# New PSUM banks for the last pair's sums, and three engines instead of two on mixer B's first queries

## The chip, the cores and the metric

The kernel runs on one core of one Trainium2 chip. The metric is the device time of one execution in microseconds (us); the median of several runs counts. The engines are TensorE (PE, matrix products, with its weight loads shown as PEld), VectorE (DVE), ScalarE (ACT), GpSimd (POOL) and SyncE (SP, which here issues the weight DMAs). Every engine works through its own queue in order and waits there for the other engines.

## The reference

Two layers of an encoder over 256 tokens of width 2048: layer 0 with mixer A (grouped-query attention), layer 1 with mixer B (three groups of heads with windows and dilations), each followed by a gated MLP of inner width 5632 with a convolution of width 3 in it, and a final norm.

```
def reference(x, ...):
    h = x
    for i in range(DEPTH):                      # 2
        hn = rms_norm(h, mix_norm[i])
        h = h + (mixer_a if i % 2 == 0 else mixer_b)(hn, ...)
        h = h + conv_ffn(rms_norm(h, ffn_norm[i]), w_up[i], conv_w[i], conv_b[i], w_down[i])
    return rms_norm(h, final_norm)

def mixer_b(h, w_qkv, w_o, rel_bias):           # 3 groups of 8 heads of 128
    qkv = (h @ w_qkv).reshape(b, s, 3, 3, 8, 128)
    for g in range(3):
        o, lz = dilated_group(q[g], k[g], v[g], rel_bias[g], window[g], dilation[g])
        ...
    return concat(softmax(log_zs)[g] * outs[g]) @ w_o

def conv_ffn(h, w_up, conv_w, conv_b, w_down):
    gate, val = split(depthwise_conv3(h @ w_up) + conv_b)
    return (silu(gate) * val) @ w_down
```

## The kernel before

All weights stream from HBM in blocks of 128 x 1024 float32 (`raw`, loaded from SP's queue, six buffers). Products are made in PE's reduced float32 format with a high and a low part: `split_raw` has ACT round a block to its high half `wh` (line 128) and DVE subtract it for the low half `wl` (line 129); both sit in a short ring of buffers. Each block is used by matmuls with `wh` and then with `wl`, so that PE needs a `wh` when it begins a block and a `wl` some matmuls later. The activations stand on the other side in the same two parts.

**Accumulators.** PSUM has eight banks of 128 x 512 float32, called b0 to b7. Some of the products are made by a seven-product scheme (Strassen-like) over two column blocks n0 and n1 and the two halves of 128 tokens: `project_pair` takes a list of `units`, one per weight block, either ("c", ...), a common block that goes into two of the four sums C11, C21 (column block n0) or C12, C22 (n1), or ("P", ...), one of the seven products. Products 1, 5, 6, 7 have accumulators of their own, M1, M5, M6, M7, and are added by `combine` on DVE and ACT (lines 475 to 487); products 2, 3 and 4 go straight into C11, C12 and C21. At the end `done` adds C11, C21 and then C12, C22 to the residual stream `h` (line 649). Which bank each of the eight takes is written out in `project_pair` (lines 221 to 223): the i-th name of `place` takes the i-th bank of the list, and b is the same for consecutive pairs.

```
            place = ("M1", "M5", "M6", "M7", "C11", "C21", "C12", "C22")
            b = bank_at[0]
            acc = {k: bank((4, 5, 6, 7, 2 - b, 3 - b, b, b + 1)[i], "acc") for i, k in enumerate(place)}
```

The last MLP (layer 1) does its down-projection in two halves `hf` over the inner width; in the second, `pair(0, 1, ...)` and then `pair(2, 3, ..., tail=True)` are the last matmuls of the program. The units of the tail begin with four common blocks that go into C11 and C21, then product 1, and C12 and C22 come late. A new tile in a bank waits for the last reader of the tile before it.

**Mixer B's queries.** Each half `hf` of the heads (four heads of every group) goes through groups g = 0, 1, 2. `seven` makes keys and queries with the same scheme; `k_gen` and `s_gen` are generators that are advanced one piece at a time between the weight blocks, so their instructions are interleaved with the block splits in the queues of ACT, DVE and POOL. For the queries, ACT scales the sums into `stg` (line 797), DVE turns 32 x 32 blocks in `tT` (line 348), and `place_blocks` puts sixteen pieces of 32 x 256 where they belong: the letter of `place` for each of four partition groups says which engine copies (p is POOL, line 358; a is ACT, line 360; v is DVE, line 362). For group 0 the placed queries are then split into `qTh` (ACT, line 303) and `qTl` (DVE, line 304) for the score matmuls.

A scheduler sets the final order within each queue; block splits have priority over what surrounds them.

Of the kernel before, what the change touches and what calls it, by code (L numbers as in the profile page):

```python
# [33 lines left out]
def tile_encoder(ctx: ExitStack, tc: tile.TileContext, x, xT, w_a, w_ao, q_gain, k_gain, w_b, w_bo,  # L34
# [180 lines left out]
    def project_pair(w, n0, n1, lhs, forms, units, late, early_done, n0_done, product_done=None, tail=False,  # L215
                     lazy=False):
        home = {1: "M1", 2: "C11", 3: "C12", 4: "C21", 5: "M5", 6: "M6", 7: "M7"}
        if product_done or lazy:
            acc = dict(zip(("C11", "C21", "C12", "C22"), new_acc() + new_acc()))
        else:  # L220
            place = ("M1", "M5", "M6", "M7", "C11", "C21", "C12", "C22")
            b = bank_at[0]
            acc = {k: bank((4, 5, 6, 7, 2 - b, 3 - b, b, b + 1)[i], "acc") for i, k in enumerate(place)}

        def touched(u):
            return (home[u[2]],) if u[0] == "P" else (("C11", "C21"), ("C12", "C22"))[u[2] // 2]

        first, last = {}, {}
        for i, u in enumerate(units):
            for k in touched(u):  # L230
                first.setdefault(k, i)
                last[k] = i
        if tail:
            last["C12"] = last["C22"] = None
        blocks = {}
        sums = {5: ("11", "12"), 7: ("12", "22"), 6: ("22", "11"), 4: ("21", "22")}

        def block(kg, b):
            if (kg, b) not in blocks:
                blocks[kg, b] = load_raw(w, (n0, n1)[int(b[1]) - 1], kg, int(b[0]) - 1)  # L240
            return blocks[kg, b]

        def prepare(u):
            kind, kg, p = u
            if kind == "P" and p in sums:
                dst, src = (block(kg, b) for b in sums[p])
                with tc.high_priority(offset=AHEAD):
                    nc.vector.tensor_tensor(dst, dst, src, ALU.add)  # L248
                if p == 6:
                    done_raw(blocks.pop((kg, "11")))  # L250
                elif p == 4:
                    done_raw(blocks.pop((kg, "22")))

        last_s = max(i for i, u in enumerate(units) if u[0] == "P")
        for i, (kind, kg, p) in enumerate(units):
            if i == late:
                drain()
            if kind == "c":
                r = load_raw(w, (n0, n1)[p // 2], kg, p % 2)
            else:  # L260
                b = {1: "11", 2: "21", 3: "22", 5: "11", 7: "12", 6: "22", 4: "21"}[p]
                r = block(kg, b)
            if i + 1 < len(units):
                prepare(units[i + 1])
            wh, wl = split_raw(r, kind == "c" or p in (7, 4))
            if kind == "P" and p in (7, 4):
                blocks.pop((kg, b))
            todo = []
            if kind == "c":
                for j in range(2):  # L270
                    for m, k in enumerate(touched((kind, kg, p))):
                        todo.append((k, *at(lhs[4 * kg + 2 * (p % 2) + j], m), j))
            else:
                f = forms(kg)[p]
                for j in range(2):
                    x = f[j] if isinstance(f, list) else [t[:, j * P:(j + 1) * P] for t in f]
                    todo.append((home[p], *x, j))
            for k, *_ in todo:
                if k not in acc:
                    acc[k] = bank(4 + ("M1", "M5", "M6", "M7").index(k), "acc") if lazy else ps_tile()  # L280
            fresh = {k for k in acc if first[k] == i}
            for k, xh, xl, j in todo:
                nc.tensor.matmul(acc[k], xh, wh[:, j, :], start=k in fresh, stop=False)  # L283
                fresh.discard(k)
                nc.tensor.matmul(acc[k], xl, wh[:, j, :], start=False, stop=False)  # L285
            todo.sort(key=lambda t: (t[0], t[3]))
            for k, xh, xl, j in todo:
                nc.tensor.matmul(acc[k], xh, wl[:, j, :], start=False, stop=last[k] == i and j == 1)  # L288
            if product_done and kind == "P" and home[p][0] == "M":
                product_done(home[p], acc.pop(home[p]))  # L290
            if i == last_s:
                early_done(acc)
            if i == max(last["C11"], last["C21"]):
                n0_done(acc)
            if not (product_done or lazy) or kind == "c" or p in (1, 5, 7, 4):
                step()
        return acc
# [521 lines left out]
    def heads_T_dve(o, s, pool, tag, place="pava", more=False):  # L819
        hi, lo = o  # L820
        dst = hi if lo is None else s.rearrange("p m c -> p (m c)").rearrange("p (j t) -> p j t", j=4)
        yield from turned(dst, s, pool, tag, place)
        yield
        if more:
            yield
        if lo is not None:
            split(hi, lo, dst)
# [209 lines left out]
    def mixer_b(hT, ss_in):  # L1037
        with tc.tile_pool(name="bpool", bufs=1) as bp:
# [26 lines left out]
            for hf in range(2):  # L1065
# [15 lines left out]
                def s_gen(g, accs, bts, nmx=nmx, lsum=lsum, nmv=nmv, probs=probs, e=e, kTs=kTs):  # L1081
                    qs = evac_scaled(bp, accs, rstd)
                    yield
                    yield
                    kT, qT = kTs[g], pair_tile(bp, [P, 4, NT], "qT", 1, g > 0)
                    yield from heads_T_dve(qT, qs, bp, "vl", "papa", g == 0)
                    W = NT if g == 0 else P
                    if g < 2:
                        yield
                    for i in range(4):  # L1090
                        yield
                        s = ps_tile()
                        for m in range(2):
                            ks_ = (allp, i) if g == 0 else (allp, i, slice(m * P, (m + 1) * P))
                            mm3(s[:, m * W:(m + 1) * W], qT, kT, (allp, i, slice(m * P, (m + 1) * P)), ks_,
                                True, True)
                        lg = bp.tile([P, 2, NT], F32, tag="lg", name=nm("lg"), bufs=2)
                        lgv = lg[:, :, :W]
                        b = bts[i] if g == 0 else bts[i][:, None, :].to_broadcast([P, 2, P])
                        nc.vector.scalar_tensor_tensor(lgv, s[:, :2 * W].rearrange("p (m c) -> p m c", m=2),  # L1100
                                                       SCALE, b, ALU.mult, ALU.add)
                        nc.vector.tensor_reduce(nmv[:, g, :, i], lgv, axis=AX.X, op=ALU.max, negate=True)
                        sl = (2 * g + 1) * 4 + i
                        if g == 0:
                            pr = [hpool.tile([P, NT], F32, tag=f"a{c}{sl}", name=nm("pr")) for c in "hl"]
                        else:
                            pt = hpool.tile([P, NT], F32, tag=f"ah{sl}", name=nm("pr"))
                            pr = [pt[:, :P], pt[:, P:], pt]
                        for m in range(2):
                            c = 4 * m + i  # L1110
                            nc.scalar.activation(pr[m], lg[:, m, :W], AF.Exp, bias=nmx[:, g, c:c + 1],
                                                 accum_out=lsum[:, g, c:c + 1])
                        probs.append(pr)
                    if g < 2:
                        return
                    mn = small.tile([P, 8], F32, tag="mn", name=nm("mn"))
                    nc.vector.tensor_tensor(mn, nmx[:, 0, :], nmx[:, 1, :], ALU.min)
                    nc.vector.tensor_tensor(mn, mn, nmx[:, 2, :], ALU.min)
                    nc.vector.tensor_tensor(e, mn[:, None, :].to_broadcast([P, 3, 8]), nmx, ALU.subtract)
                    nc.scalar.activation(e, e, AF.Exp)  # L1120
                    nc.vector.tensor_tensor(lsum, lsum, e, ALU.mult)
                    nc.vector.tensor_tensor(mn, lsum[:, 0, :], lsum[:, 1, :], ALU.add)
                    nc.vector.tensor_tensor(mn, mn, lsum[:, 2, :], ALU.add)
                    nc.vector.reciprocal(mn, mn)
                    nc.vector.tensor_tensor(e, e, mn[:, None, :].to_broadcast([P, 3, 8]), ALU.mult)
# [219 lines left out]
```

## Time and profile before

| | us |
|---|---|
| median of 3 runs | 2241.69 (2239.77 to 2242.25) |
| profiled execution, its own time | 2239.69 |
| span of that execution, first to last instruction | 2237.8 |
| PE busy in it | 2223.3 |

A row of a timeline gives start and duration in us, engine, line, operation, output<-inputs, sizes and a count of like instructions in a row; in square brackets is the time for which the engine sat idle before it and what ended that. A row of the waits gives the waiting instruction, what it waited for, and the total, the number and the longest of these waits.

### The profile page before, as it was taken

Reading aid. Unit: us, or ns where it says so; the run is one execution under the profiler, and the core shown is the slowest. Engines: PE = TensorE matmul, PEld = TensorE weight load, DVE = VectorE, ACT = ScalarE, POOL = GpSimd, SP = SyncE. Lnnn points to the kernel's source line nnn. Section 1 sums busy time; section 2 is a strip of 40 time slices with the busy share of each in tenths; the row PEclk is TensorE's granted clock in tenths of the full one; section 3 lists DMA queues with packets and bytes.
Section 4 is the critical chain, followed back from the end, with each engine's and each line's share of the span. In section 5 each row is a group of like instructions: output and inputs, shape, how many; then the busy total and the mean of one; then the engine's idle time right before and its main releaser. Section 6 shows DMA issues by size and latency. Waiting matters only on the chain.

```text
span 2237.8 us, 29101 instructions
## 1 busy us (share of the span) xinstructions
PE 2223.3 (99%) x10033; PEld 1841.7 (82%) x10033; DVE 1806.2 (81%) x2461; ACT 1540.7 (69%) x2373; POOL 339.6 (15%) x490
## 2 busy tenths in 40 slices
PE   9999999999999999999999999999999999999998
PEld 7888888888888888888888888888888888888886
DVE  6777778888878788979887888786887898688897
ACT  7665677777547777767876777576777755677764
POOL 2210212210001010012431313010110100001110
PEclk9999999999999999999999999999999999999999
DMA  8444657766655655666555565565665666555654
GB/s 302 164 146 152 207 189 207 246 200 190 216 196 188 199 188 179 227 203 214 197 185 187 163 206 178 187 199 190 192 194 193 193 207 207 188 193 193 225 190 140
DMA packets 126499, 437.43 MB, mean 195 GB/s; under 512 B 17312, under 2 KB 18080, under 8 KB 126352
## 3 DMA queue, kind: packets, MB, share of 16 engines
q1 hardware_dynamic: 119744, 425.64, 57.9%
q0 software_dynamic: 6176, 9.39, 1.7%
q8 instruction: 78, 1.28, 0.2%
q14 instruction: 69, 0.57, 0.1%
q10 hardware_dynamic: 432, 0.56, 0.1%
HBM read 429.20 MB, written 6.29 MB: 195 GB/s over the span
## 4 chain that ended last, share of the span: by engine, by line
PE 93%; DVE 2%; POOL 2%; issue 1%; ACT 1%; DMA 1%; SPq 0%; DVEq 0%; POOLq 0%; ACTq 0%
PE acc L154 19%; PE acc L155 19%; PE acc L153 19%; PE acc L283 10%; PE acc L285 10%; PE acc L288 10%; POOL stg L358 1%; DVE wl L129 1%; PE ps L318 1%; PE ps L322 0%; POOL pp L358 0%; PE ps L321 0%; PE ps L320 0%; ACT wh L128 0%; PE ps L285 0%
## 5 line engine op out<-in xcount | busy, mean ns | idle before, releaser
L129 DVE TENSOR_TENSOR wl<-raw,wh 128x1024 fp32r<-128x1024 f32 x855 | 1051.5, 1236 | 298.2 <-ACT wh L128 294.7
L128 ACT ACTIVATE wh<-raw 128x1024 fp32r<-128x1024 f32 x855 | 899.3, 1057 | 489.3 <-PE acc L155 198.9
L154 PE MATMUL acc<-wl,xh 128*128 128x512 f32 x1792 | 698.1, 390 | 0.7 <-DVE wl L165 0.4
L153 PE MATMUL acc<-wh,xh 128*128 128x512 f32 x1792 | 698.5, 390 | 0.1
L155 PE MATMUL acc<-wh,xh 128*128 128x512 f32 x1792 | 697.8, 389 | 0.0
L154 PEld LDWEIGHTS acc<-wl,xh 128*128 128x128 f32 x1792 | 336.5, 188 | 71.4 <-DVE wl L165 1.7
L155 PEld LDWEIGHTS acc<-wh,xh 128*128 128x128 f32 x1792 | 336.4, 188 | 69.5
L153 PEld LDWEIGHTS acc<-wh,xh 128*128 128x128 f32 x1792 | 336.4, 188 | 69.0 <-ACT wh L164 0.5
L283 PE MATMUL acc<-wh,ah 128*128 128x512 f32 x762 | 296.9, 390 | 1.5 <-DVE h L649 1.5
L285 PE MATMUL acc<-wh,al 128*128 128x512 f32 x762 | 296.7, 389 | 0.0
L358 POOL COPY u<-t 32x256 f32<-32x256 f32 x176 | 110.9, 630 | 1003.4 <-DVE t L540 995.3
L288 PE MATMUL acc<-wl,ah 128*128 128x512 f32 x762 | 211.8, 389 | 0.0
L283 PEld LDWEIGHTS acc<-wh,ah 128*128 128x128 f32 x762 | 143.0, 188 | 31.6 <-DVE h L649 1.9
L288 PEld LDWEIGHTS acc<-wl,ah 128*128 128x128 f32 x762 | 143.0, 188 | 29.7
L285 PEld LDWEIGHTS acc<-wh,al 128*128 128x128 f32 x762 | 143.0, 188 | 29.5
L360 ACT ACTIVATE u<-t 32x256 f32<-32x256 f32 x352 | 147.7, 420 | 14.0 <-DVE t L540 6.2
L283 PE MATMUL acc<-wh,xh 128*128 128x512 f32 x312 | 122.4, 392 | 1.1 <-ACT wh L128 1.1
L285 PE MATMUL acc<-wh,xh 128*128 128x512 f32 x312 | 121.5, 390 | 0.0
L248 DVE TENSOR_TENSOR raw<-raw,raw 128x1024 f32<-128x1024 f32 x84 | 103.4, 1231 | 12.3 <-DMA raw<-in_w_down_dram 11.5
L288 PE MATMUL acc<-wl,xh 128*128 128x512 f32 x312 | 84.9, 390 | 0.0
L154 PE MATMUL acc<-wl,ah 128*128 128x512 f32 x216 | 84.2, 390 | 0.3 <-DVE wl L129 0.3
L153 PE MATMUL acc<-wh,ah 128*128 128x512 f32 x216 | 84.2, 390 | 0.0
(244 smaller groups left out, 2264.8 us busy)
## 6 DMA issues: line engine op xcount, KB each, us to landing
raw<-in_w_up_dram SPq DMA_DIRECT2D x352, 512.0 KB, 4.4
raw<-in_w_down_dram SPq DMA_DIRECT2D x176, 512.0 KB, 4.8
raw<-in_w_b_dram SPq DMA_DIRECT2D x144, 512.0 KB, 4.5
raw<-in_w_bo_dram SPq DMA_DIRECT2D x48, 512.0 KB, 4.5
raw<-in_w_a_dram SPq DMA_DIRECT2D x40, 512.0 KB, 4.5
raw<-in_w_ao_dram SPq DMA_DIRECT2D x32, 512.0 KB, 3.8
raw<-in_w_a_dram SPq DMA_DIRECT2D x16, 256.0 KB, 6.2
h<-in_x_dram SPq DMA_DIRECT2D x4, 512.0 KB, 8.4
```

The source lines that it names most:

```text
L128: nc.scalar.activation(wh, r, AF.Copy)
L129: nc.vector.tensor_tensor(wl, r, wh.bitcast(F32), ALU.subtract)
L153: nc.tensor.matmul(accs[m], xh, wh[:, j, :], start=st, stop=False)
L154: nc.tensor.matmul(accs[m], xh, wl[:, j, :], start=False, stop=False)
L155: nc.tensor.matmul(accs[m], xl, wh[:, j, :], start=False, stop=sp)
L248: nc.vector.tensor_tensor(dst, dst, src, ALU.add)
L283: nc.tensor.matmul(acc[k], xh, wh[:, j, :], start=k in fresh, stop=False)
L285: nc.tensor.matmul(acc[k], xl, wh[:, j, :], start=False, stop=False)
L288: nc.tensor.matmul(acc[k], xh, wl[:, j, :], start=False, stop=last[k] == i and j == 1)
L318: nc.tensor.matmul(o, lh[ls], rh[rs], start=start, stop=stop)
L358: nc.gpsimd.tensor_copy(dst, src)
L360: nc.scalar.activation(dst, src, AF.Copy)
```

## The change

Two edits. In the tail pair the eight names take the banks in another order: C11, C12, C21, C22 go to b4 to b7, where the pair before kept M1, M5, M6, M7, and the products M1, M5, M6, M7 go to the banks that held C11, C21, C12, C22. And for group 0 of mixer B the queries' placement is "pava" instead of "papa": four of the eight pieces that POOL copied are copied by DVE, in each half of the heads.

```
             place = ("M1", "M5", "M6", "M7", "C11", "C21", "C12", "C22")
+            if tail:
+                place = ("C11", "C12", "C21", "C22", "M1", "M5", "M6", "M7")
             b = bank_at[0]
...
                     kT, qT = kTs[g], pair_tile(bp, [P, 4, NT], "qT", 1, g > 0)
-                    yield from heads_T_dve(qT, qs, bp, "vl", "papa", g == 0)
+                    yield from heads_T_dve(qT, qs, bp, "vl", "papa" if g else "pava", g == 0)
```

All line numbers after line 221 grow by two. SP's order is unchanged.

The first places are in PE's queue, at the start of the tail pair. The accumulators acc_19562 to acc_19569 are created in the order of `place`, so that before the change 19562 is M1, 19566 C11 and 19567 C21:

```order
L283 MATMUL acc_19566<-wh_19572,ah_17520 128x512
L285 MATMUL acc_19566<-wh_19572,al_17521 128x512
L283 MATMUL acc_19566<-wh_19572,ah_17522 128x512
L285 MATMUL acc_19566<-wh_19572,al_17523 128x512
L283 MATMUL acc_19567<-wh_19572,ah_17520 128x512
L285 MATMUL acc_19567<-wh_19572,al_17521 128x512
```

In the same place after the change 19562 is C11 and 19564 is C21:

```order
L285 MATMUL acc_19562<-wh_19572,ah_17520 128x512
L287 MATMUL acc_19562<-wh_19572,al_17521 128x512
L285 MATMUL acc_19564<-wh_19572,ah_17520 128x512
L287 MATMUL acc_19564<-wh_19572,al_17521 128x512
L285 MATMUL acc_19562<-wh_19572,ah_17522 128x512
L287 MATMUL acc_19562<-wh_19572,al_17523 128x512
```

C21's first matmul moved from the fifth to the third place of the block.

The second place is DVE's queue in the first half of the heads, from the turning of group 0's queries (stg_9266 are the queries, tT_9318 their turned blocks) to the low half qTl_9317. Before:

```order
L348 STREAM_TRANSPOSE tT_9318<-stg_9266 128x512 x2
L129 TENSOR_TENSOR wl_9350<-raw_9347,wh_9349 128x1024
L304 TENSOR_TENSOR kTl_9208<-stg_9186,kTh_9207 128x1024
L129 TENSOR_TENSOR wl_9372<-raw_9369,wh_9371 128x1024
L248 TENSOR_TENSOR raw_9347<-raw_9347,raw_9401 128x1024
L129 TENSOR_TENSOR wl_9390<-raw_9387,wh_9389 128x1024
L129 TENSOR_TENSOR wl_9405<-raw_9399,wh_9404 128x1024
L248 TENSOR_TENSOR raw_9401<-raw_9401,raw_9466 128x1024
L129 TENSOR_TENSOR wl_9423<-raw_9347,wh_9422 128x1024
L304 TENSOR_TENSOR qTl_9317<-stg_9266,qTh_9316 128x1024
```

After:

```order
L350 STREAM_TRANSPOSE tT_9318<-stg_9266 128x512 x2
L364 COPY stg_9266<-tT_9318 32x8x32 x2
L129 TENSOR_TENSOR wl_9350<-raw_9347,wh_9349 128x1024
L306 TENSOR_TENSOR kTl_9208<-stg_9186,kTh_9207 128x1024
L129 TENSOR_TENSOR wl_9372<-raw_9369,wh_9371 128x1024
L129 TENSOR_TENSOR wl_9390<-raw_9387,wh_9389 128x1024
L250 TENSOR_TENSOR raw_9347<-raw_9347,raw_9401 128x1024
L129 TENSOR_TENSOR wl_9405<-raw_9399,wh_9404 128x1024
L364 COPY stg_9266<-tT_9318 32x8x32 x2
L250 TENSOR_TENSOR raw_9401<-raw_9401,raw_9466 128x1024
L129 TENSOR_TENSOR wl_9423<-raw_9347,wh_9422 128x1024
L306 TENSOR_TENSOR qTl_9317<-stg_9266,qTh_9316 128x1024
```

Four copies came in, two at the start and two ahead of the last sum of blocks, and wl_9390 moved ahead of one such sum. ACT's queue is the same as before here.

The third place is DVE's queue in the second half of the heads (stg_11194 are the queries). Before, wl_11318 follows wl_11300:

```order
L248 TENSOR_TENSOR raw_11275<-raw_11275,raw_11329 128x1024
L129 TENSOR_TENSOR wl_11300<-raw_11297,wh_11299 128x1024
L129 TENSOR_TENSOR wl_11318<-raw_11315,wh_11317 128x1024
L304 TENSOR_TENSOR qTl_11245<-stg_11194,qTh_11244 128x1024
L129 TENSOR_TENSOR wl_11333<-raw_11327,wh_11332 128x1024
```

After:

```order
L250 TENSOR_TENSOR raw_11275<-raw_11275,raw_11329 128x1024
L129 TENSOR_TENSOR wl_11300<-raw_11297,wh_11299 128x1024
L364 COPY stg_11194<-tT_11246 32x8x32 x4
L129 TENSOR_TENSOR wl_11318<-raw_11315,wh_11317 128x1024
L306 TENSOR_TENSOR qTl_11245<-stg_11194,qTh_11244 128x1024
```

All four copies came in between these two. POOL's queue has four copies instead of eight at both places. Between the first place's queries and the next group a few more instructions swap neighbours on DVE and ACT (a row maximum and a low half, an exponential and a block split).

## The prediction

> **What bounds the kernel now.** I read the page first (engine totals, clock row), then the engine's waits, then the timelines around each wait.
>
> ```profile
> PE 2223.3 (99%) x10033; PEld 1841.7 (82%) x10033; DVE 1806.2 (81%) x2461; ACT 1540.7 (69%) x2373; POOL 339.6 (15%) x490
> PEclk9999999999999999999999999999999999999999
> PE acc L283 <- DVE h L649: 1.5, 1, 1.5
> PE acc L283 <- ACT wh L128: 1.1, 2, 1.0
> PE ps L322 <- DVE qTl L304: 0.6, 1, 0.6
> PE acc L154 <- DVE wl L129: 0.5, 2, 0.3
> ```
>
> TensorE (PE) is busy 2223.3 of a span of 2237.8 us at a full granted clock. Nothing makes the kernel shorter except fewer matmuls, which this change doesn't bring, or shorter waits of PE. The last four rows are PE's waits (total, times, longest). The first, 1.5 us, is what the bank edit speaks to; the second, 1.1 us in two places, is what the placement edit speaks to. The other two are elsewhere (the qTl one is mixer A's). So the change can't win more than a few microseconds, and the question is whether the two waits go in full and whether the work moved to VectorE (DVE) makes a new one.
>
> **The bank edit.** It moves no instruction between engines; it renames where eight accumulators live in the last pair of the second layer's second down-projection half. C11, the first sum that PE starts there, and C21, the second, are named acc_19566 and acc_19567 before, acc_19562 and acc_19564 after (the rows of PE's order are shown with the change). The products still start at the fifth weight block; only the first four blocks' sums sit in other banks, and C21 now starts at once behind C11. The timeline of PE and DVE at that place:
>
> ```profile
> 2174.68 0.39 PE L283 MATMUL acc<-wh,ah 128*128 128x512 f32 x1
> 2174.91 0.39 PE L285 MATMUL acc<-wh,al 128*128 128x512 f32 x1
> 2176.76 0.50 PE L283 MATMUL acc<-wh,ah 128*128 128x512 f32 x1 [1.47 <-DVE h L649]
> 2177.11 0.40 PE L285 MATMUL acc<-wh,al 128*128 128x512 f32 x1
> 2170.17 0.68 DVE L478 TENSOR_TENSOR cu<-acc,cu 128x512 f32<-128x512 f32 x1
> 2176.04 0.67 DVE L649 TENSOR_TENSOR h<-acc,h 128x512 f32<-128x512 f32 x1
> 2180.63 0.68 DVE L649 TENSOR_TENSOR h<-acc,h 128x512 f32<-128x512 f32 x1
> 2190.28 2.35 DVE L129 TENSOR_TENSOR wl<-raw,wh 128x1024 fp32r<-128x1024 f32 x2
> 2186.91 0.39 PE L283 MATMUL acc<-wh,ah 128*128 128x512 f32 x1
> 2194.17 1.07 PE L288 MATMUL acc<-wl,ah 128*128 128x512 f32 x4
> ```
>
> Matmuls start 0.23 us apart (2174.68, 2174.91). C21's first starts 1.85 after its predecessor, 1.62 too many, and the next follows by 0.35, 0.12 too many: 1.74 us. It waits for the L649 at 2176.04, which reads the preceding pair's C21, whose bank it takes. After the change C21 takes the bank of that pair's M6, last read by L478, which ends at 2170.85, almost 4 us before PE comes there. What is late next? M1, M5, M6 and M7 now take the banks of the old C11, C21, C12, C22, the last of which is read by the L649 that ends at 2181.31; M1, the first of the four, starts at 2186.91, 2185.2 in the new time, so nothing waits. The low halves wl that PE needs next are ready early: the tightest in this stretch ends at 2191.50 (2190.28, two in 2.35, 1.22 each, so the first at 2190.28 + 1.22) and PE comes to it at 2194.17, 2.67 later, more than the 1.74 by which PE moves up. Gain 1.74; at least the 1.47 idle that the row itself shows. I take 1.74.
>
> **The placement edit, first half of the heads.** A quarter of the sixteen-block placement of group 0's queries changes hands: 4 of POOL's 8 copies go to DVE, in each half of the heads. ACT's 8 and SP's queue stay as they are; POOL's next issue is a bias DMA that waits for DVE's use of the old bias long after. By the order shown with the change, in DVE's queue
> two copies stand ahead of all eight tensor-tensor steps that end with wl_9423, a low half that PE waits for, and two ahead of the last two of these.
>
> ```profile
> 1018.83 4.54 POOL L358 COPY stg<-tT 32x256 f32<-32x256 f32 x8 [34.16 <-DVE tT L348]
> 1024.77 9.75 POOL L358 COPY stg<-tT 32x256 f32<-32x256 f32 x8 [1.40 <-DVE tT L348]
> 1030.17 2.75 DVE L129 TENSOR_TENSOR wl<-raw,wh 128x1024 fp32r<-128x1024 f32 x2
> 1034.18 1.42 DVE L129 TENSOR_TENSOR wl<-raw,wh 128x1024 fp32r<-128x1024 f32 x1
> 1036.79 2.35 DVE L129 TENSOR_TENSOR wl<-raw,wh 128x1024 fp32r<-128x1024 f32 x2
> 1032.78 1.06 ACT L128 ACTIVATE wh<-raw 128x1024 fp32r<-128x1024 f32 x1
> 1034.55 1.06 ACT L303 ACTIVATE qTh<-stg 128x1024 fp32r<-128x1024 f32 x1 [0.71 <-POOL stg L358]
> 1035.51 1.99 ACT L128 ACTIVATE wh<-raw 128x1024 fp32r<-128x1024 f32 x2
> 1035.82 0.63 PE L288 MATMUL ps<-wl,sf 128*128 128x512 f32 x2
> 1036.61 0.50 PE L283 MATMUL acc<-wh,xh 128*128 128x512 f32 x1 [0.16 <-ACT wh L128]
> 1036.94 0.39 PE L285 MATMUL acc<-wh,xh 128*128 128x512 f32 x1
> L362 DVE COPY u<-t x176: 283/378/449, 294.0 to 2126.7; 32x256 f32<-32x256 f32 x176
> 217.03 1.12 DVE L362 COPY tM<-tT 32x256 f32<-32x256 f32 x3
> 217.13 2.65 POOL L358 COPY tM<-tT 32x256 f32<-32x256 f32 x4 [42.07 <-DVE tT L348]
> ```
>
> The chain: POOL's eight copies end at 1034.52, ACT's qTh waits for them (0.71), ACT's next weight split stands behind it, and PE waits for that: 1036.61 against 1035.82 + 2 x 0.23, 0.33 too late, and 0.10 on the next start: 0.43 us. POOL's copies took 9.75 us here and 4.54 with DVE less in the way; and DVE's steps are slowed in turn: two of them 2.75 us with POOL at work (1.34 from start to start), 2.35 without (1.13), 0.21 each.
> After: DVE gets four copies of 0.378 (the median, 0.283 to 0.449), 1.51. POOL's four run two beside DVE's copies and two beside tensor-tensors, so 2 instead of 7 of these are slowed: -1.05 (only three fewer: -0.63). The first copy needn't wait for a weight split: -0.07. Net +0.39 (+0.01 to +1.10). wl_9423 ended at 1035.60, so now 1035.99, and PE wants it at 1035.82: a new wait of 0.17 and a restart of about 0.10. The old wait goes: POOL is done by about 1028.3 (1024.77, two copies at 0.43, two at 1.34), DVE's last copies about 2.3 before wl_9423's end, at 1033.7, ACT's split at 1033.84; qTh starts some 0.7 sooner and so does the split behind it. Gain 0.43 - 0.27 = 0.16, range +0.43 to -0.55.
>
> **The second half of the heads.** Here DVE has room: all four copies stand together between wl_11300 and wl_11318.
>
> ```profile
> 1228.88 8.11 POOL L358 COPY stg<-tT 32x256 f32<-32x256 f32 x8 [1.64 <-DVE tT L348]
> 1232.94 1.41 DVE L129 TENSOR_TENSOR wl<-raw,wh 128x1024 fp32r<-128x1024 f32 x1
> 1235.49 1.23 DVE L129 TENSOR_TENSOR wl<-raw,wh 128x1024 fp32r<-128x1024 f32 x1 [1.14 <-ACT wh L128]
> 1234.40 1.06 ACT L128 ACTIVATE wh<-raw 128x1024 fp32r<-128x1024 f32 x1
> 1237.02 1.06 ACT L303 ACTIVATE qTh<-stg 128x1024 fp32r<-128x1024 f32 x1 [1.55 <-POOL stg L358]
> 1237.98 1.04 ACT L128 ACTIVATE wh<-raw 128x1024 fp32r<-128x1024 f32 x1
> 1237.51 0.61 PE L288 MATMUL acc<-wl,xh 128*128 128x512 f32 x2
> 1239.07 0.50 PE L283 MATMUL acc<-wh,xh 128*128 128x512 f32 x1 [0.95 <-ACT wh L128]
> 1239.41 0.40 PE L285 MATMUL acc<-wh,xh 128*128 128x512 f32 x1
> ```
>
> PE loses 1239.07 - 1237.51 - 2 x 0.23 = 1.10 and 0.11 on the next start, 1.21. DVE idles 1.14 us from 1234.35 on, so the copies (1.51) end at 1235.86 and push wl_11318 by 0.37, to about 1237.1; PE wants it at 1237.51. POOL's four are done by 1233.3. qTh starts at 1235.9 instead of 1237.02, the split behind it starts 0.96 later and takes 1.04: 1237.9, when PE wants it at 1237.97. Gain 1.21; with copies of 0.449 the split is 0.2 late and 0.9 is left.
>
> The row at 217.03 is the nearest to this mix: three DVE copies in 1.12 us beside POOL's copies, 0.37 each, no more than the median taken. The Trainium skill speaks against this edit ("Perfetto Trace Analysis", section "Optimizing Scalar/DVE Operations"): GpSimd and VectorE share an SBUF read port, so moving work between those two might not help. By the rows the sum below is 3.1; by that rule the placement is worth nothing and it is 1.7. The trace agrees with the sharing (9.75 us against 4.54) and not with "might not help" where DVE idles.
>
> **Sum.** 1.74 + 0.16 + 1.21 = 3.1 us (1.47 + 0.9 - 0.55 = 1.8 to 1.74 + 0.43 + 1.21 = 3.4). The profiled execution took 2239.69 us, so 2236.6 for it. The runs shown, 2239.77, 2241.69 and 2242.25, lie above it; from their median it is 2238.6, from the middle of all four executions (2240.7) 2237.6. I take 2238.1, between the two (that is 2241.2 - 3.1).
>
> **Rivals.**
> - The placement gives nothing: POOL and DVE take turns, so that the queries are placed no sooner, or DVE's copies make wl late by what POOL's cost before. For it: DVE is filled without a gap in the first half; against it: its 1.14 idle in the second. Only 1.74 is left: 2241.2 - 1.74 = 2239.5.
> - The bank edit doesn't remove its wait, because another reader of a bank is late. Against it is L478's end at 2170.85. Left is 1.4: 2239.8.
> - Slower: DVE's copies are held as POOL's were beside tensor-tensors, 1.3 us each (9.75 for eight). Then 5.2 us stand in DVE's queue in either half: in the first wl_9423 is 3.9 late (5.2 - 1.05 - 0.07 less the 0.22 it had to spare), 3.5 net of the old wait; in the second the copies end at 1239.55 and qTh starts 2.5 later than now. 3.5 + 2.5 - 1.74 = 4.3 slower: 2245.5. It takes copies of some 0.8 us to outweigh the 1.74; no row of this shape on DVE is above 0.449.
>
> **Chances.** Forecast 0.65, placement worthless 0.18, bank wait kept 0.07, slower 0.05, something larger than the sum 0.05. The three runs shown lie within 0.11%, so 0.2%, 4.5 us, is about what a measurement can tell from no change. The sum alone doesn't reach it, but the median shown lies 1 us above the middle of the executions, so that the forecast can show up as over 4.5 us below it about one time in three: faster 0.65 x 0.33 + most of 0.05 = 0.25, slower 0.05, same 0.70. The range goes from 3.4 off the fastest execution, 2236.3, to the rivals that keep half the gain off the highest run, 2240.8, with 0.4 at either end for so few runs.
>
> **What would show it.** The wait for L649 is gone and C21 starts 0.23 behind C11. POOL shows 4 copies at both places, ACT's qTh idles no more for POOL, the two waits on ACT's wh are gone and a small one on wl stands in the first half. Wrong would be: DVE copies over 0.45 us, a wl wait over 0.5 at either place, or a longer tail after the last matmul.

## The result, and the profile after

| | before | after |
|---|---|---|
| median of 14 runs each | 2240.47 us | 2236.84 us |
| lowest and highest | 2238.75 to 2242.94 | 2235.73 to 2238.25 |
| profiled execution, and its span | 2239.69, 2237.8 | 2236.83, 2235.0 |

The ratio is 0.9982, 95% interval 0.9974 to 0.9989: 0.18% faster, a difference clear of the noise, and smaller than the 0.2% that the prediction took for the least that shows. It was 2238.1 predicted; 2236.84 is inside its range.

The engines' totals and PE's waits after the change (engine, line, what it waited for; total, times, longest). L649 of before is L651 now, L478 is L480, and so on: two lines came in above.

```profile
PE 2222.7 (99%) x10033; PEld 1842.6 (82%) x10033; DVE 1805.4 (81%) x2469; ACT 1540.1 (69%) x2373; POOL 330.3 (15%) x482
PE acc L154 <- DVE wl L129: 0.8, 2, 0.6
PE ps L324 <- DVE qTl L306: 0.6, 1, 0.6
```

The two waits of the prediction, for the L649 and for ACT's wh, are gone from the list; VectorE has eight instructions more (2461 to 2469) and POOL eight fewer. The timeline of PE and DVE at the tail:

```profile
2173.22 0.39 PE L285 MATMUL acc<-wh,ah 128*128 128x512 f32 x1
2173.44 0.39 PE L287 MATMUL acc<-wh,al 128*128 128x512 f32 x1
2173.67 0.39 PE L285 MATMUL acc<-wh,ah 128*128 128x512 f32 x1
2173.90 0.39 PE L287 MATMUL acc<-wh,al 128*128 128x512 f32 x1
2169.83 0.68 DVE L480 TENSOR_TENSOR cu<-acc,cu 128x512 f32<-128x512 f32 x1
2175.70 0.68 DVE L651 TENSOR_TENSOR h<-acc,h 128x512 f32<-128x512 f32 x1
2152.76 1.23 DVE L250 TENSOR_TENSOR raw<-raw,raw 128x1024 f32<-128x1024 f32 x1 [0.80 <-DMA raw<-in_w_down_dram]
```

C11's first matmul starts at 2173.22, C21's at 2173.67, 0.23 behind the one ahead of it. M6's reader (L480) was done at 2170.51. The reader of old C21 (the L651) ends at 2176.38: in this execution, in the order of before (C21 fifth, 0.91 behind C11), the old bank would have held PE for 2.3 us, not for the 1.62 in the trace of before. VectorE is later against TensorE here, and the last row shows where: it stood 0.80 us for a weight block.

The first half of the heads, POOL, DVE, ACT and PE:

```profile
1025.15 3.62 POOL L360 COPY stg<-tT 32x256 f32<-32x256 f32 x4 [1.40 <-DVE tT L350]
1025.12 0.69 DVE L364 COPY stg<-tT 32x256 f32<-32x256 f32 x2
1033.28 0.59 DVE L364 COPY stg<-tT 32x256 f32<-32x256 f32 x2
1035.04 1.22 DVE L129 TENSOR_TENSOR wl<-raw,wh 128x1024 fp32r<-128x1024 f32 x1
1034.14 1.04 ACT L305 ACTIVATE qTh<-stg 128x1024 fp32r<-128x1024 f32 x1
1036.00 0.39 PE L287 MATMUL ps<-wh,sf 128*128 128x512 f32 x1
1036.31 0.74 PE L290 MATMUL ps<-wl,sf 128*128 128x512 f32 x2
1036.89 0.40 PE L285 MATMUL acc<-wh,xh 128*128 128x512 f32 x1
```

POOL's four end at 1028.77 (1028.3 was predicted), ACT's qTh idles no more, and wl_9423 ends at 1036.26, so that PE starts 0.31 after its predecessor instead of 0.23: the small new wait.

The second half of the heads:

```profile
1229.12 4.40 POOL L360 COPY stg<-tT 32x256 f32<-32x256 f32 x4 [1.64 <-DVE tT L350]
1234.63 1.18 DVE L364 COPY stg<-tT 32x256 f32<-32x256 f32 x4
1235.85 1.23 DVE L129 TENSOR_TENSOR wl<-raw,wh 128x1024 fp32r<-128x1024 f32 x1
1235.93 1.06 ACT L305 ACTIVATE qTh<-stg 128x1024 fp32r<-128x1024 f32 x1 [0.22 <-DVE stg L364]
1236.90 1.04 ACT L128 ACTIVATE wh<-raw 128x1024 fp32r<-128x1024 f32 x1
1237.76 0.62 PE L290 MATMUL acc<-wl,xh 128*128 128x512 f32 x2
1238.22 0.40 PE L285 MATMUL acc<-wh,xh 128*128 128x512 f32 x1
```

qTh waits 0.22 for VectorE instead of 1.55 for POOL, the split behind it ends at 1237.94, and PE takes it at 1238.22 without a wait.

TensorE issues the same 10033 matmuls in both kernels, so each one's start, less its start in the trace of before, says where time was won. Where that offset moves (times of before):

| place | offset ahead | behind | won |
|---|---|---|---|
| program start to 925.9 | 0.00 | 0.06 | -0.06 |
| 926.6, L154 waits for a low half (a place that the change leaves alone) | 0.06 | 0.40 | -0.34 |
| 1035.8 to 1036.9, first half of the heads | 0.40 | 0.18 | 0.22 |
| 1239.1 to 1239.4, second half | 0.25 | -0.96 | 1.21 |
| 2176.8 to 2177.1, tail | -1.01 | -2.76 | 1.75 |

The three places give 3.18, where the prediction's terms give 3.11, and stretches that the change doesn't touch take 0.4 back; between the places the offset drifts by less than 0.1. The medians differ by 3.63. Is that chance, or is a term larger than its one profiled execution shows?

### The profile page after: what moved, and what is told of

Read it like the earlier page. It is cut to its first block, busy times and chain, and to the rows that moved or that the text cites. A ratio compares the mean times of both kernels' runs of the same rounds, so it can differ in the third digit from the quotient of the medians.

```text
span 2235.0 us, 29102 instructions
## 1 busy us (share of the span) xinstructions
PE 2222.7 (99%) x10033; PEld 1842.6 (82%) x10033; DVE 1805.4 (81%) x2469; ACT 1540.1 (69%) x2373; POOL 330.3 (15%) x482
## 4 chain that ended last, share of the span: by engine, by line
PE 96%; DVE 2%; issue 1%; POOL 1%; DMA 1%; ACT 0%; SPq 0%; DVEq 0%; POOLq 0%; ACTq 0%
PE acc L154 19%; PE acc L155 19%; PE acc L153 19%; PE acc L285 11%; PE acc L287 11%; PE acc L290 11%; PE ps L320 1%; DVE wl L129 1%; PE ps L290 0%; PE ps L287 0%; PE ps L285 0%; PE ps L324 0%; POOL pp L360 0%; PE ps L323 0%; PE ps L322 0%
## 5 line engine op out<-in xcount | busy, mean ns | idle before, releaser
L154 PE MATMUL acc<-wl,xh 128*128 128x512 f32 x1792 | 698.0, 390 | 0.6 <-DVE wl L165 0.3
L154 PEld LDWEIGHTS acc<-wl,xh 128*128 128x128 f32 x1792 | 336.5, 188 | 70.5 <-DVE wl L129 1.3
L154 PE MATMUL acc<-wl,ah 128*128 128x512 f32 x216 | 84.2, 390 | 0.6 <-DVE wl L129 0.6
```

The costliest lines, as they stand in the source:

```text
L154: nc.tensor.matmul(accs[m], xh, wl[:, j, :], start=False, stop=False)
```

## Experiments

### Each edit alone

The bank edit alone puts `"papa"` back for all groups:

```
-yield from heads_T_dve(qT, qs, bp, "vl", "papa" if g else "pava", g == 0)
+yield from heads_T_dve(qT, qs, bp, "vl", "papa", g == 0)
```

> Only the bank edit; the queries stay half on POOL, half on ACT at both places. My theory: C21 of the last pair starts 0.23 us behind its predecessor, PE's wait on the L651 (L649 before) that reads the preceding pair's C21 is gone, and this alone brings 1.74 us of the changed kernel's; PE's two waits on ACT's wh beside the queries stay as before (0.16 and 0.95 idle). Span 2237.8 - 1.7 = 2236.1. Rival, that the two edits hang together (work that VectorE took over shifts it against TensorE until the end): the tail gains less than 1.2 or more than 2.2 us without the placement.

It took 2238.44 (median of 11) against 2241.09 for before on the same chip, ratio 0.9985 (0.9976 to 0.9994), span 2236.4. Its trace wins 1.75 at the tail, as expected, and nothing at the other two places. PE's wait for the old bank is gone and the second half's is there:

```profile
PE acc L285 <- ACT wh L128: 0.9, 1, 0.9
```

But the medians differ by 2.65, almost a microsecond more than the 1.7. The interval of the ratio, 1.3 to 5.4 us, holds both numbers, so that the medians alone can't settle it.

The placement alone keeps the last pair's banks:

```
-if tail:
+if False:
```

> Only the placement edit; the last pair's banks as before. My theory: TensorE gains 0.2 us at the first half of the heads and 1.2 at the second, and then keeps the tail's wait for the reader of old C21; span 2237.8 - 1.4 = 2236.4. Rival 1, that the gain is given back at the tail: if VectorE doesn't move up with TensorE there, the tail's wait grows from 1.5 by what was gained, up to 2.9, and the span stays at 2237.8. Rival 2, that moving work between GpSimd and VectorE is worth nothing: PE's waits on ACT's wh at the two places are as before.

It took 2240.01, 1.08 less than before, ratio 0.9995 (0.9986 to 1.0004), an interval that includes no change at all, span 2238.2. In the trace the two places won 0.23 and 1.2, as expected. At the tail the first rival came true in part (PE, DVE):

```profile
2177.20 0.50 PE L285 MATMUL acc<-wh,ah 128*128 128x512 f32 x1 [2.37 <-DVE h L651]
2153.53 1.23 DVE L250 TENSOR_TENSOR raw<-raw,raw 128x1024 f32<-128x1024 f32 x1 [1.03 <-DMA raw<-in_w_down_dram]
```

The wait grew from 1.47 to 2.37 and ate 0.9. So the wait isn't a constant: VectorE stood 1.03 us for weights here, and 0.12 in the profile of before. Is that an effect of the placement, or does it differ from execution to execution?

### The same programs once more

The kernel before and the placement alone, unchanged, profiled a second time.

> The kernel before once more, profiled a second time. The placement alone showed a tail wait of 2.4 us in place of 1.5, with VectorE's readers later against TensorE. My theory: that is no effect of the placement but differs from execution to execution of one program, with when VectorE gets its weights by DMA in the pair before; then the tail's wait here is another than 1.5, by 0.2 us or more, and the span above 2237.8 where it is longer. Rival, that the wait is fixed by the program: 1.5 again within 0.1.

> The placement edit alone, profiled a second time. If the tail's wait is set by the execution, it is another than 2.4 us, by 0.2 or more, and VectorE shows another idle time for a weight block's DMA in the pair before; if the placement's gain is given back there by the program, it is 2.4 again, or 1.4 + 0.9 = 2.3 within 0.1. The gains at the two places stay 0.2 and 1.1 either way.

Before a second time: one time of 2241.72, span 2239.9. PE, DVE, and PE's granted clock (the stretches of time: us, busy time and count of PE, PEld, DVE, ACT and POOL, PEclk, DMA share, GB/s):

```profile
2174.90 0.39 PE L285 MATMUL acc<-wh,al 128*128 128x512 f32 x1
2177.30 0.73 PE L283 MATMUL acc<-wh,ah 128*128 128x512 f32 x1 [2.01 <-DVE h L649]
2177.82 0.63 PE L285 MATMUL acc<-wh,al 128*128 128x512 f32 x1
2178.25 0.63 PE L283 MATMUL acc<-wh,ah 128*128 128x512 f32 x1
2153.62 1.23 DVE L248 TENSOR_TENSOR raw<-raw,raw 128x1024 f32<-128x1024 f32 x1 [0.65 <-DMA raw<-in_w_down_dram]
2173.99:2177.40 3.41, 1.40 (x7) 0.85 (x5) 3.41 (x7) 0.71 (x2) 0.00 (x0) 1.00 0.88 305
2177.40:2180.81 3.41, 3.41 (x8) 2.65 (x9) 3.41 (x4) 2.02 (x4) 2.05 (x1) 0.50 0.36 115
```

The placement alone a second time: 2241.21, span 2239.4.

```profile
2176.72 0.50 PE L285 MATMUL acc<-wh,ah 128*128 128x512 f32 x1 [2.13 <-DVE h L651]
2153.05 1.22 DVE L250 TENSOR_TENSOR raw<-raw,raw 128x1024 f32<-128x1024 f32 x1 [0.78 <-DMA raw<-in_w_down_dram]
2174.58:2177.99 3.41, 1.27 (x7) 1.05 (x6) 3.41 (x6) 0.72 (x2) 0.49 (x1) 1.00 0.75 280
2177.99:2181.40 3.41, 3.41 (x10) 2.64 (x9) 3.41 (x5) 1.78 (x3) 3.06 (x2) 0.50 0.45 150
```

Two things follow. First, one program shows waits of 1.47 and 2.01, the other 2.37 and 2.13: the execution sets the wait. Over thirteen traces the end of old C21's reader, counted from C11's first matmul, goes with the time that VectorE stood for weights between 2152 and 2156 (the half dose, and C21 on M7's bank, have two such idles each, and the sum is given):

| trace | VectorE idle for DMA | reader's end behind C11's start | 2.36 + idle |
|---|---|---|---|
| second half only (two traces) | 0 | 2.36, 2.35 | 2.36 |
| before | 0.12 | 2.49 | 2.48 |
| all four pieces on ACT | 0.32 | 2.71 | 2.68 |
| bank edit alone | 0.42 | 2.78 | 2.78 |
| no copies on POOL | 0.58 | 2.96 | 2.94 |
| before, again | 0.65 | 3.02 | 3.01 |
| placement alone, again | 0.78 | 3.15 | 3.14 |
| after | 0.80 | 3.16 | 3.16 |
| placement alone | 1.03 | 3.39 | 3.39 |
| after, again | 1.12 | 3.49 | 3.48 |
| half dose | 1.17 | 3.63 | 3.53 |
| C21 on M7's bank | 0.33 | 2.79 | 2.69 |

All agree within 0.03 but the two with two idles, which are 0.10 longer. It is a relation seen across executions: no run here moved that transfer on purpose, and why it lands late in some isn't shown.

Second, in both of these executions TensorE's granted clock fell to 0.50 after the wait, for 3.41 us and some eight matmuls that start 0.43 apart (2177.82 to 2178.25) instead of 0.23. By the offsets that costs 1.5 us in either (0.53 to 2.07, and -0.04 to 1.50). So the old bank cost 1.74 us in the profile that I predicted from, 2.6 in the first of the placement alone, and 3.8 and 3.95 in the two executions here (by the offsets 2.07 more than 1.74 in before again, and 2.21 more in the other).

The Trainium skill ("TensorE: Matmul & The Clock Gate", section "Part 1: The HAM clock gate") has the clock halve after at least one idle window of some 3.4 us, the windows running freely. The length of the window agrees: the clock stood at 0.50 for 3.41 us in either trace (2177.40 to 2180.82, 2177.99 to 2181.40), and in all thirteen traces the clock's changes lie a whole number of 3.413 us apart. It doesn't agree that the whole window has to be idle, and the measurement decides: in the last window before the drop PE was still busy for 1.40 of 3.41 us in one trace and for 1.27 in the other. An idle of 2.37, longer than either, left the clock at 1.00 in the first profile of the placement alone. Counted from the changes of its clock, the border of two windows falls into that idle, at 2176.73, and the emptier of the two still has PE busy for 1.51:

```profile
2173.32:2176.73 3.41, 1.51 (x7) 0.93 (x5) 3.41 (x6) 0.79 (x1) 0.00 (x0) 1.00 0.84 287
2176.73:2180.14 3.41, 2.94 (x13) 2.45 (x14) 3.41 (x5) 2.35 (x5) 2.06 (x1) 1.00 0.34 121
```

These three traces fit a rule by which the idle time within one window tells, with a limit between 1.40 and 1.51 of PE's busy time, and by which it is chance where the borders fall. The other ten traces don't contradict it, but no run moved a border or an idle on purpose.

### A later reader for the new bank

The bank edit with C21 and C22 exchanged, so that C21 takes M7's bank:

```
-place = ("C11", "C12", "C21", "C22", "M1", "M5", "M6", "M7")
+place = ("C11", "C12", "C22", "C21", "M1", "M5", "M6", "M7")
```

> The bank edit with one name exchanged, without the placement: C21, the second sum to start, takes the bank of the preceding pair's M7, which VectorE reads one instruction ahead of old C21 (0.59 us earlier in the trace of before), instead of that of M6, read some 5 us earlier. My theory, that only the time of the bank's last reader counts: a wait of PE on VectorE comes back at C21's first matmul, 1.0 us long as VectorE stood in the trace of before (2176.12 + 0.05 against 2175.14), so that of the 1.74 only about 0.6 is left (span 2237.2); up to 1.7 and nothing left if VectorE stands as in the trace of the changed kernel. Rival, that the gain comes from the new order of the banks as such or from other readers: no wait there, and a span as with the bank edit alone, 2236.1.

It took 2240.73, 0.36 less than before, ratio 0.9999 (0.999 to 1.0007): nothing is left, the lower end of what was expected.

```profile
2176.66 0.50 PE L285 MATMUL acc<-wh,ah 128*128 128x512 f32 x1 [1.63 <-DVE cu L488]
```

The wait is back, now for the reader of M7. C21 starts 1.79 later than it would without a wait, 0.76 more than the 1.03 worked out first: C21 comes third behind C11's start here, as in the changed kernel, where before has it fifth (0.46 of it), and VectorE was 0.30 later (2.79 against 2.49 in the table). New names alone bring nothing; the bank's last reader has to lie well ahead.

The spread of the runs says the same. The kernels with the old bank or M7's go over 4 to 5 us (before 2239.38 to 2244.08 in 33 runs, placement alone 2238.25 to 2243.37, this one 2239.08 to 2243.49, 11 runs each), with standard deviations of 1.4; the bank edit alone spans 1.5 us (2237.92 to 2239.45), 0.5. The granted clock of the single runs points the same way. Its mean is 0.998 or less in 28 of the 81 runs of before that stand beside these experiments, and in 9 of 22 with the placement alone or M7's bank, but in only 4 of the 91 runs of kernels in which C21 has M6's bank; among the 33 runs of before here the median is 2242.71 with the lower clock and 2240.19 without. The mean is rounded and holds the lower clock behind the last matmul too, so it counts the drops only roughly.

### The first half of the heads left as before

```
-"papa" if g else "pava"
+"papa" if g or hf == 0 else "pava"
```

> The changed kernel with the first half of the heads as before (eight copies on POOL, eight on ACT); the second half keeps four on VectorE. My theory, that in the first half the placement wins 0.43 and loses about 0.2 by a late wl, net 0.2: PE's wait on ACT's wh is back there (0.16 idle, 0.43 in all), none on wl, and the span is 0.2 above the changed kernel's: 2235.2. The second half still gains 1.2, the tail 1.74. Rival, that the first half carries more of the gain through VectorE's later work: the second half's wait comes back or the tail's gain changes, and the span is over 0.6 above.

It took 2236.97 against 2241.09, ratio 0.9982 (0.9973 to 0.9991), span 2234.9: no slower than the changed kernel, whose profile it undercuts by 0.1. The second half won 1.23 and the tail 1.75. The 0.2 of the first half isn't missed. The next run asked where it goes.

### No copies on POOL, and the four pieces on ACT

`"vava"` for group 0 (eight copies on VectorE, eight on ACT), and `"paaa"` (four on POOL, twelve on ACT):

> The changed kernel with POOL out of the placement: all eight of its copies of group 0's queries on VectorE, eight on ACT. The scheduler then puts ACT's split wh_9436 ahead of qTh in the first half, wh_11332 ahead of qTh in the second, and VectorE's wl_9423 ahead of an addition. My theory: beside POOL a copy is slow and slows VectorE's two-input steps (1.34 apart against 1.13), and alone VectorE's copies take 0.29 us, so eight cost 2.3 us in either half and nothing waits: no PE wait at either place, span about 0.2 below the changed kernel's, 2234.8. Rival, VectorE is full there: wl_9423 or the splits behind come 1 us or more late, PE waits on wl, span 2236 or more.

> The changed kernel with the four pieces on ACT instead of VectorE (four on POOL, twelve on ACT, none on VectorE). My theory: what counts is only that POOL has half as many, since POOL's copies ended last; ACT's take 0.42 us each, 1.7 in either half, and the scheduler lets the weight splits past them: PE's waits at both places stay under 0.3, span within 0.4 of the changed kernel's, 2235.0. Rival, that it takes VectorE's idle time, and ACT, which also makes wh and qTh, is late by the 1.7 us: PE waits on ACT's wh 0.5 us or more in either half as before, span 2236.0 or more.

Both theories fell. Without POOL it took 2239.21 against 2241.25, ratio 0.999 (0.9981 to 0.9999); with ACT 2239.47, 0.9991 (0.9983 to 1.0): about half the gain each. (The spans, 2237.5 and 2238.1, lie higher than that, since 1.0 and 1.3 us were lost at 926, a place that none of these edits touches.) At the first half itself the expectation for the former held: VectorE's copies take 0.29 each, and PE's next matmul with a low half starts 0.22 behind its predecessor.

```profile
1033.10 1.18 DVE L364 COPY stg<-tT 32x256 f32<-32x256 f32 x4
1036.41 0.39 PE L287 MATMUL ps<-wh,sf 128*128 128x512 f32 x1
1036.63 0.62 PE L290 MATMUL ps<-wl,sf 128*128 128x512 f32 x2
```

The loss is 41 us behind it, and again 43 us behind the second half, where group 1's queries are placed:

```profile
1077.41 0.50 PE L285 MATMUL acc<-wh,xh 128*128 128x512 f32 x1 [0.20 <-ACT wh L128]
1078.67 0.72 PE L290 MATMUL acc<-wl,xh 128*128 128x512 f32 x2
1281.17 0.50 PE L285 MATMUL acc<-wh,xh 128*128 128x512 f32 x1 [0.27 <-ACT wh L128]
```

Against the changed kernel PE loses 0.87 at the first of these and 1.0 at the second. With the pieces on ACT it loses 0.9 at 1077, and 1.0 just behind the second half, where qTh and the splits around it come later (PE idles 0.45 for a wl there).

What PE takes 41 us behind the first half is the low half wl_9816. How long it was ready ahead:

| first half of the heads | traces | wl_9816 ready ahead of PE |
|---|---|---|
| as before | before, before again, bank edit alone, second half only (two) | 0.76, 0.73, 0.76, 0.76, 0.73 |
| four copies to VectorE | after, after again, placement alone, again | 0.34, 0.29, late, late |
| two to VectorE (half dose, below) | one | 0.40 |
| eight to VectorE; four to ACT | one each | late, late |

The way there leads over ACT. Before and after:

```profile
1062.88 1.71 ACT L360 ACTIVATE kT<-tT 32x256 f32<-32x256 f32 x4 [0.67 <-DVE tT L348]
1075.35 2.56 DVE L129 TENSOR_TENSOR wl<-raw,wh 128x1024 fp32r<-128x1024 f32 x2 [1.58 <-ACT wh L128]
1063.51 1.70 ACT L362 ACTIVATE kT<-tT 32x256 f32<-32x256 f32 x4 [0.66 <-DVE tT L350]
1075.98 2.56 DVE L129 TENSOR_TENSOR wl<-raw,wh 128x1024 fp32r<-128x1024 f32 x2 [1.60 <-ACT wh L128]
```

VectorE turns group 1's keys later, ACT waits for that and starts to place them 0.63 later by the clock of the trace, 0.43 later against PE, which is 0.20 behind there. From then on ACT works without a gap up to the split that wl_9816 is made from, and VectorE itself idles 1.6 us for that split. Not all of the 0.43 need be the copies' own time: in the order that the scheduler makes with four or more pieces moved VectorE also idles 0.27 for a split of ACT at about 1052, which no trace of the old order shows, and no run separates the two.

So the edit takes some 0.4 from a spare of 0.76, and where something else is late as well, PE waits: 0.14 in the placement alone, and 0.7 in its second profile, in which ACT stood 4.28 us for a weight block at 1043.95 (2.60 in the changed kernel).

```profile
1077.73 0.74 PE L290 MATMUL acc<-wl,xh 128*128 128x512 f32 x2 [0.28 <-DVE wl L129]
```

### Changed kernel, second half only, and half a dose, side by side

The half dose gives VectorE two of the four pieces in the first half of the heads, POOL six; everything else is as in the changed kernel:

```
-if place[b] == "p":
+if (place * 2)[b + i // 8 * 4] == "p":
...
-"papa" if g else "pava"
+"papa" if g else "pava" if hf else "pavapapa"
```

> The changed kernel once more, beside the next two on one chip. My theory after the runs so far: the tail has no wait however late VectorE is there, so its times spread over less than 3 us (those of before over 5); in the first half of the heads it gains 0.2 and gives 0 to 0.6 back 40 us later, where VectorE, 0.4 later than without the first half's edit, makes wl_9816 late for PE in some executions. Rival: the spread and the later wait are of the chip's day and not of the program.

> The changed kernel with the first half of the heads as before, second run. My theory: the first half's edit is worth nothing, since what it gains (0.2) goes again 40 us later; so the median is within 0.4 of the changed kernel's beside it, and wl_9816 is ready 0.7 to 0.8 ahead of PE. Rival, the first half's 0.2 counts in full: 0.2 or more slower than the changed kernel.

> A half dose in the first half of the heads: two copies on VectorE instead of four (six on POOL); the second half and the banks as in the changed kernel. ACT's and VectorE's orders 40 us later are those of before again. My theory: POOL still ends some 2 us sooner than with eight, so that the wait on ACT's wh (0.43) is gone; wl_9423 is no later than PE wants it; and VectorE is late by at most 0.2 at wl_9816, so nothing comes back there: 0.2 to 0.5 faster than the changed kernel and the one with the second half only, the best of the three. Rival: two copies leave POOL's end too late, and the wait of 0.43 stays; then it equals the one with the second half only.

| | median of 11 | lowest, highest | ratio to before (95%) |
|---|---|---|---|
| before (27 runs) | 2241.09 | 2239.51, 2245.28 | |
| changed kernel | 2237.18 | 2236.37, 2239.41 | 0.9981 (0.9972 to 0.999) |
| second half only | 2237.27 | 2236.27, 2238.25 | 0.9982 (0.9973 to 0.9991) |
| half dose | 2236.65 | 2235.47, 2237.44 | 0.9976 (0.9967 to 0.9985) |

The changed kernel's spread is 3.04, just over the 3 expected and half of before's 5.77. The first half's edit is worth nothing in the medians, 0.09, which 11 runs of each can't tell from the 0.2 of the rival. The trace of the second half only has wl_9816 ready 0.73 ahead, as expected, and in that of the changed kernel, with 0.29, nothing came back. The profile of the second half only has span 2236.4, not by the change: PE waited longer for a low half at 926, a place that none of these edits touches and where the traces of this study differ by 1.4 us from one execution to another.

```profile
PE acc L154 <- DVE wl L129: 1.5, 2, 1.2
```

The half dose came out lowest by 0.5, within what 11 runs of each can't separate for certain. Its trace shows why it can be better and why it isn't by more (POOL, DVE, PE):

```profile
1025.37 6.30 POOL L360 COPY stg<-tT 32x256 f32<-32x256 f32 x6 [1.40 <-DVE tT L350]
1034.25 1.23 DVE L250 TENSOR_TENSOR raw<-raw,raw 128x1024 f32<-128x1024 f32 x1 [0.37 <-DMA raw<-in_w_b_dram]
1036.21 0.39 PE L287 MATMUL ps<-wh,sf 128*128 128x512 f32 x1
1036.67 0.73 PE L290 MATMUL ps<-wl,sf 128*128 128x512 f32 x2
```

POOL's six are done at 1031.67, early enough for qTh, so the wait of 0.43 is gone with half the copies. But a weight block landed late, VectorE stood 0.37, and PE waited for the same low half, 0.33; the place won 0.10. At 1077 wl_9816 was 0.40 ahead, less than the 0.55 at least that I expected (0.76 less 0.2); the 0.37 of the late block is as much as is missing from 0.76.

## Why the prediction was right, and where it was off

- **Bank edit, 1.74.** The mechanism was right, and in the profiled execution so was the size: 1.75. As the term of a sum for the median it was too small. The prediction took the length of a wait from one execution and treated it as the program's. It was 1.47 to 2.37 us, going with the time that VectorE stood for a weight block some 20 us ahead, and 1.5 more where the clock dropped after it. Alone the edit moved the median by 2.65, and its interval, 1.3 to 5.4, leaves open how much of the surplus is this. The rows of one profile couldn't show it; the runs' spread of 0.11%, 2239.77 to 2242.25, was read as noise of the measurement, and the edit alone brought the standard deviation from 1.4 to 0.5, so most of it hangs on this wait. What made the transfer late stays open.
- **First half, 0.16 (+0.43 to -0.55).** At the place 0.22, and 0.22 in the second trace. The new wait for wl_9423 was 0.20 where 0.27 was expected. The step that failed is "what is late next": the prediction stopped at the first wait behind the edit, and 41 us on VectorE's lateness, carried over by ACT, meets a spare of 0.76. In the profile of the changed kernel nothing came back there, so the 0.16 agrees with the 0.22; over the runs the edit is worth nothing that can be measured: 2237.18 with it, 2237.27 without.
- **Second half, 1.21.** 1.21, and 1.21 to 1.23 in the six other traces with this edit. The split was ready at 1237.94 as worked out (1237.9).
- **The copies, 0.378 each.** 0.34 for the first pair, beside POOL's (0.69 for two), 0.29 to 0.30 for the others (1.18 for four); the median row taken was that of other copies of this shape. Too dear by 0.05 to 0.1 each, which changed nothing.
- **Sum and forecast.** 3.1 against 3.63 in the medians here, 3.91 in the second comparison. 2238.1 was 1.3 too high: 0.5 of it from the sum, most likely its bank term, and 0.7 from the base, 2241.2, where 14 runs of before have 2240.47. The sum on the profiled execution alone gave 2236.6, and that of the changed kernel took 2236.83. So close an agreement is partly luck: in another execution of before the old bank cost 2.1 us more, and at 926 the executions differ by as much as 1.4.
- **Rivals.** That the placement is worth nothing fell: it won 1.2 at the second half in every trace. The median by itself moved by 1.08, with an interval that includes no change. The Trainium skill's sentence behind that rival ("Perfetto Trace Analysis", "Optimizing Scalar/DVE Operations"), that moving work between GpSimd and VectorE might not help, agrees with the first half (0.09), though there the delay came back by way of ACT and no run shows the port to be the cause, and not with the second, where VectorE idled. That the bank edit keeps its wait came true only with M7's bank. That the copies take 1.3 us on VectorE fell: 0.3.

## What to carry to other kernels

A wait that ends in a DMA some instructions back has no one length: read it in two or three profiled executions, and look at the spread of the times, before its removal is priced. Moving work onto a nearly full engine can be paid far behind the place, here 41 us later and by way of another engine, so follow the delay from engine to engine to where the smallest spare is, not just to the next wait; half a dose of the move removed the same wait. Where sums take over banks, those that start first belong in banks whose last reader is long done: with a bank read some 5 us earlier than the old one C21 didn't wait, with one read 0.6 us earlier it did.

## What was not expected of the hardware

After waits of 2.01 and 2.13 us TensorE ran at a granted clock of 0.50 for 3.41 us, some eight matmuls, with 1.5 us lost besides the wait; a wait of 2.37 in another execution didn't do this, and lay across the border of two such stretches of 3.41 us. A copy of 32x256 costs VectorE 0.29 us where POOL is done and 0.34 beside POOL's copies.
